# A three-branch encoder layer on eight cores: packed layouts, balanced token blocks, projections run between attention steps

## The chip, the cores and the metric

The kernel runs on the 8 cores of one Trainium2 chip (two dies: cores 0 to 3 and 4 to 7). Each core computes one batch element; nothing is exchanged between cores. The metric is the device time in microseconds of the slowest core. A program on all cores has a second, slower state in some executions, in which the cores of one die (or both) show a lower granted TensorE clock; only fast executions are compared here.

## The reference, cut to what matters

```python
D_MODEL, SEQ, DEC_SEQ, PAST_LEN = 2048, 2048, 64, 1024      # 2048 prompt + 64 sample tokens per core
# input projection columns: fox q,k,v, forget logits, fox gate, conv B, C, h, conv gate, mem q, mem gate
z = jnp.einsum('btd,dn->btn', x, w_in)
# A) forgetting attention, 12 heads x 128
s = jnp.einsum('bqhd,bkhd->bhqk', qi, k) * scale + ci[..., :, None] - cum[:, :, None, :]
s = jnp.where(k_pos[None, :] <= pi[:, None], s, NEG_INF)
o = jnp.einsum('bhqk,bkhd->bqhd', jax.nn.softmax(s, axis=-1), v)
# B) gated causal convolution of width 3, 1536 channels, and its last two inputs as a state output
# C) cross-attention of 4 heads x 256 to 256 memory tokens
# each branch * silu(gate) -> its output matrix; merged by sigmoid gates of x; then W_o and LayerNorm
m = g1 * y_fox + g2 * y_conv + g3 * y_mem
return _layernorm(DN_ALPHA * x + jnp.einsum('btd,de->bte', m, w_o), ln_g, ln_b)
```

The outputs are also the new K, V and log-forget caches and the convolution state (two tokens of 1536 channels, for prompt and sample).

## The kernel before

Heads run one after the other: all projections of a head, then its attention. Each attention tile is a score matmul, on the diagonal a mask matmul, an addition on VectorE, an exponential on ScalarE, a value matmul and a matmul with ones that sums the rows.

```python
TBLK = [(0, 512), (512, 512), (1024, 512), (1536, 512), (2048, 64)]
...
    for h in range(nheads):
        ...  # K, V, Q and gate projections of head h, K transposes
        def issue_S(i):
            ...
            S.add(PE, MM(banks[sb_][0:kn, n0:qn], kl, qT[:, qcol0 + n0:qcol0 + qn], True, not diag),
                  reads=rds + [r_qT[tbidx]], writes=[bankr[sb_]])
            if diag:
                S.add(PE, MM(banks[sb_][0:kn, n0:n0 + kn], identb[0:kn, 0:kn], masknegb[0:kn, 0:kn], False, True),
                      reads=[r_const], writes=[bankr[sb_]])
            ...
        def issue_PV(i):
            ...
            S.add(PE, MM(banks[Ob][:, n0:qn], vv, pt[p][0:kn, n0:qn], first, last),
                  reads=[r_pt[p]] + rds, writes=[bankr[Ob]])
            S.add(PE, MM(banks[Lb][:, n0:qn], onesb[0:kn, :], pt[p][0:kn, n0:qn], first, last),
                  reads=[r_pt[p], r_const], writes=[bankr[Lb]])
```

Second, the end of the convolution stores the state with four transfers whose elements lie 4 bytes at a time in memory; the merge bias is loaded in such a way at the start.

```python
    S.add(SP, DMA(bm[:], I["b_merge"].rearrange("(c p) o -> p (c o)", p=128), allow_slow_non_contiguous=True),
          writes=[r_const], dmasem=dconst)
...
        for j in range(2):
            S.add(SP, DMA(O["cv_p"][j:j + 1, :].rearrange("o (c p) -> p (o c)", p=128), utail[:, j, :],
                          allow_slow_non_contiguous=True), reads=[r_ut], dmasem=d_ut)
            S.add(SP, DMA(O["cv_s"][j:j + 1, :].rearrange("o (c p) -> p (o c)", p=128), ustail[:, j, :],
                          allow_slow_non_contiguous=True), reads=[r_ut], dmasem=d_ut)
```

Each stage allocates its own weight buffers from memory that the stage before releases, and x is loaded with tokens along the partitions and transposed on TensorE.

The softmax here doesn't subtract the row's maximum and nothing guards it: scores larger than these inputs give would overflow.

## Time and profile before

4072.21 us median of three fast runs (4066.46 to 4072.93; a fourth, 4310.36, is slow). The profiled execution had a slow second die, so all is read on core 0 of the undisturbed die, 4045.0 us. The prediction below shows the lines. To them I add an account of core 0: for every matmul, the time from its start to the next start, less columns/2.4 + 2.5 ns (29.4 ns for 64 columns and fewer), the cost that the dense stretches show. What is left over is sorted by its size: a start-to-start of 1.5 to 2.3 times the cost counts as a matmul at half clock, more than that as a wait. The sort goes by size alone and is rough: of the 18.3 us of half clock after, only 7.4 stand where the trace grants half clock (91.5 of the 97.4 before); the rest are short waits.

| core 0, us | before | after |
|---|---|---|
| until the first matmul | 26.0 | 10.5 |
| issue cost of all matmuls | 3390.0 | 3271.7 |
| waits | 511.5 | 61.4 |
| half clock | 97.4 | 18.3 |
| other | 2.4 | 6.3 |
| after the last matmul's start | 17.7 | 17.0 |
| span | 4045.0 | 3385.2 |

### The profile page before, as it was taken

The page shows a single profiled execution, that of the slowest core. Times are in us where ns is not written, and L with a number is a line of the kernel's source. Part 1 is how long each engine was busy: PE and PEld are TensorE (multiplying, and loading weights), DVE is VectorE, ACT ScalarE, POOL GpSimd, SP SyncE. Part 2 cuts the span into 40 slices and gives each one's busy share as a digit, 9 for nine tenths or more (in the row PEclk, how much of TensorE's full clock was granted, in tenths as well). Part 3 has the DMA queues.
Part 4 walks back from the last instruction along what each step waited for, and adds up shares of the span by engine and source line. Part 5 has one row for each costly group of instructions (what it writes and reads, how often), then busy time and mean ns, then how long its engine had stood idle before and what let it go on. Part 6 is the DMA issues. An engine that isn't in the chain of part 4 may idle for free.

```text
span 4605.7 us, 57539 instructions; the slowest of 8 cores (4037.3 to 4605.7 us)
## 1 busy us (share of the span) xinstructions
PE 4112.2 (89%) x20854; PEld 1977.5 (43%) x20854; DVE 840.7 (18%) x1331; ACT 1033.7 (22%) x1840; POOL 786.6 (17%) x675
## 2 busy tenths in 40 slices
PE   4888888888888799999999998599997997999898
PEld 2555545555555344444444443244443443444343
DVE  2222222222221100101111111000000221111254
ACT  2444433444443110111111111011112331111111
POOL 1111111111110000002132131122210111222122
PEclk7999978999997788888888887688877887888787
DMA  8333333333331433632442440955835203665532
GB/s 102 50 53 60 52 43 52 52 52 52 52 52 34 60 63 66 86 43 21 35 37 19 37 33 4 65 106 105 142 86 75 30 8 55 110 121 115 182 132 92
DMA packets 500443, 303.11 MB, mean 66 GB/s; under 512 B 275440, under 2 KB 457456, under 8 KB 494140
## 3 DMA queue, kind: packets, MB, share of 16 engines
q0 software_dynamic: 344080, 134.54, 29.1%
q1 hardware_dynamic: 156088, 164.89, 12.7%
q8 instruction: 174, 2.85, 0.3%
q14 instruction: 101, 0.83, 0.1%
HBM read 345.03 MB, written 88.88 MB: 94 GB/s over the span
## 4 chain that ended last, share of the span: by engine, by line
PE 85%; ACT 5%; DMA 4%; issue 3%; DVE 2%; another core or an unknown queue 1%; DVEq 0%; ACTq 0%; SPq 0%; POOL 0%; POOLq 0%
PE bank L146 84%; ACT rl_92 L163 1%; DMA xb_14_56<-xp 1%; DMA mwb_74_116<-w_in 1%; DMA wm_56_98<-w_merge 0%; PE bank L152 0%; DMA mwb_74_116<-w_mem_kv 0%; DMA wm_107_149<-w_merge 0%; DVE st_41_83 L181 0%; ACT pt_47_89 L163 0%; ACT pt_44_86 L163 0%; ACT pt_45_87 L163 0%; ACT pt_49_91 L163 0%; ACT pt_48_90 L163 0%
## 5 line engine op out<-in xcount | busy, mean ns | idle before, releaser
L146 PE MATMUL bank<-xT_55,cwb_52_94 128*128 128x512 bf16 (+1 forms) x1920 | 418.8, 389 | 3.2 <-ACT scg_114 L163 1.8
L146 PE MATMUL bank<-xT_55,cwb_53_95 128*128 128x512 bf16 (+1 forms) x1920 | 418.8, 389 | 3.2 <-ACT scg_114 L163 2.2
L146 PE MATMUL bank<-wbuf_69,xT_55 128*128 128x256 bf16 (+1 forms) x3264 | 403.5, 290 | 16.1 <-ACT kv_1_34_76 L168 10.7
L146 PE MATMUL bank<-xT_55,wbuf_69 128*128 128x512 bf16 (+1 forms) x1920 | 360.7, 350 | 17.8 <-ACT kT_71 L168 8.5
L146 PEld LDWEIGHTS bank<-wbuf_69,xT_55 128*128 128x128 bf16 (+1 forms) x3264 | 337.3, 104 | 76.5 <-issue 21.6
L146 PE MATMUL bank<-wob_146,mT_159 128*128 128x512 bf16 (+1 forms) x1088 | 287.6, 438 | 21.5 <-DMA mT_159<-m_scrb 21.5
L146 PEld LDWEIGHTS bank<-xT_55,cwb_52_94 128*128 128x128 bf16 x1920 | 180.8, 107 | 240.8 <-issue 240.6
L146 PEld LDWEIGHTS bank<-xT_55,cwb_53_95 128*128 128x128 bf16 x1920 | 180.8, 107 | 240.6 <-issue 240.6
L146 PEld LDWEIGHTS bank<-xT_55,wbuf_69 128*128 128x128 bf16 x1920 | 165.1, 99 | 209.2 <-issue 60.5
L146 PE MATMUL bank<-xT_55,wm_79_121 128*128 128x512 bf16 (+1 forms) x640 | 147.6, 393 | 69.0 <-DMA wm_79_121<-w_merge 69.0
L146 PEld LDWEIGHTS bank<-wob_146,mT_159 128*128 128x128 bf16 (+1 forms) x1088 | 119.5, 110 | 189.1 <-issue 179.2
L146 PE MATMUL bank<-qT_70,kT_71 128*128 128x512 bf16 (+4 forms) x492 | 189.3, 392 | 9.9 <-ACT kcT_81 L168 9.5
L146 PE MATMUL bank<-xT_55,wm_56_98 128*128 128x512 bf16 (+1 forms) x640 | 147.1, 392 | 24.0 <-DMA wm_56_98<-w_merge 24.0
L146 PE MATMUL bank<-xT_55,wm_107_149 128*128 128x512 bf16 (+1 forms) x640 | 147.2, 392 | 23.3 <-DMA wm_107_149<-w_merge 23.3
L163 ACT ACT_TABLE_LOAD x69 | 88.5, 1283 | 328.1 <-PE bank L146 265.1
L173 POOL TENSOR_TENSOR aT_68<-on_93,sg_73 128x512 bf16<-128x512 f32 (+1 forms) x60 | 64.7, 1078 | 553.9 <-DVE on_93 L173 409.8
L146 PE MATMUL bank<-xT_55,mwb_74_116 128*128 128x512 bf16 (+1 forms) x640 | 142.3, 392 | 12.6 <-DMA mwb_74_116<-w_in 10.3
L146 PE MATMUL bank<-xT_55,wm_57_99 128*128 128x512 bf16 (+1 forms) x640 | 145.5, 389 | 0.0
L146 PE MATMUL bank<-xT_55,wm_80_122 128*128 128x512 bf16 (+1 forms) x640 | 145.5, 389 | 0.0
L146 PE MATMUL bank<-xT_55,wm_108_150 128*128 128x512 bf16 (+1 forms) x640 | 145.5, 389 | 0.0
L173 DVE TENSOR_TENSOR up_111<-bank,cg_110 128x512 f32<-128x512 f32 x48 | 33.2, 692 | 611.0 <-PE bank L146 611.0
L146 PE MATMUL bank<-xT_55,mwb_75_117 128*128 128x512 bf16 (+1 forms) x640 | 140.7, 389 | 2.3 <-ACT mqT_137 L168 2.3
(277 smaller groups left out, 4856.6 us busy)
## 6 DMA issues: line engine op xcount, KB each, us to landing
wbuf_69<-w_in POOLq DMA_DIRECT2D x48, 512.0 KB, 12.8
cqb_74<-cum_scr SPq DMA_DIRECT2D x12, 1024.0 KB, 5.6
cwb_52_94<-w_in POOLq DMA_DIRECT2D x24, 512.0 KB, 18.2
cwb_53_95<-w_in POOLq DMA_DIRECT2D x24, 512.0 KB, 17.9
m_scr<-mt_60_102 SPq DMA_DIRECT2D x32, 256.0 KB, 2.1
m_scr<-mt_61_103 SPq DMA_DIRECT2D x32, 256.0 KB, 2.0
pv_85_127<-m_scr SPq DMA_DIRECT2D x32, 256.0 KB, 3.6
pv_86_128<-m_scr SPq DMA_DIRECT2D x32, 256.0 KB, 4.3
```

What stands on the lines that cost most here:

```text
L146: return lambda e: e.matmul(out, lhsT=lhsT, rhs=rhs, start=start, stop=stop)
L163: return lambda e: e.activation(out=out, in_=in_, func=func, **kw)
L173: return lambda e: e.tensor_tensor(out=out, in0=in0, in1=in1, op=op)
```

## The change

The intent: keep TensorE fed all the time. The diff replaces most of the kernel; this is its core, with cuts marked by dots and comments added.

```diff
-TBLK = [(0, 512), (512, 512), (1024, 512), (1536, 512), (2048, 64)]
+TB = [(0, 424), (424, 424), (848, 424), (1272, 420), (1692, 420)]
...
-    ("cv_p", [2, FW]), ("mk_p", [MT, MW]), ("mv_p", [MT, MW]), ("fk_s", [NS, FW]), ("fv_s", [NS, FW]),
-    ("b_merge", [3 * D, 1], F32), ("w_o", [D, D], F32), ("ln_g", [1, D], F32), ("ln_b", [1, D], F32),
+    ("w_mem_out", [16, 128, 8, 128], F32), ("w_merge", [48, 128, 16, 128], F32), ("b_merge", [128, 48], F32),
...
+    def load_next(si):                       # eight weight slots, filled in the order of use
+        key, src, nk = stream[spos[0]]
+        ...
+    for q in range(4):                       # prologue: token block 0 and the first K weights in quarters
+        S.add(POOL, DMA(xT[0][:, 4 * q:4 * q + 4, :], I["xT0"][:, 4 * q:4 * q + 4, :]), writes=[r_xT[0][q]], ...)
+        S.add(POOL, DMA(slots[0][0][:, 4 * q:4 * q + 4, :], stream[0][1][:, 4 * q:4 * q + 4, :]), ...)
...
-            if diag:
-                S.add(PE, MM(banks[sb_][0:kn, n0:n0 + kn], identb[0:kn, 0:kn], masknegb[0:kn, 0:kn], False, True), ...)
+        def fmask():                         # the mask is added to the forget row once, on GpSimd
+                S.add(POOL, TT(m[:, :]..., t[:, :]..., masknegb..., ALU.add), ...)
...
-            S.add(PE, MM(banks[Lb][:, n0:qn], onesb[0:kn, :], pt[p][0:kn, n0:qn], first, last), ...)
+            S.add(DVE, TT(ac[0:kn, n0:n], ac[0:kn, n0:n], p[0:kn, n0:n], ALU.add), reads=[rac, rp], writes=[rac])
+    # at the end of a query block: high and low bf16 parts on GpSimd, two matmuls with ones
+        def f2():
+            bk, rb = PJ.next()
+            E.pe(MM(bk[:, 0:n], onesb[:, :], hi[:, 0:n], True, False), n, [rhi, r_const], [rb])
+            E.pe(MM(bk[:, 0:n], onesb[:, :], lo[:, 0:n], False, True), n, [rlo, r_const], [rb])
...
+    for h in range(H):
+            F.add(*[g_v(h + 1, b) for b in range(5)])     # and K, Q, gate projections of head h + 1
+        for s in ss:
+            step(s)                          # one attention tile of head h
+            F.run(fill * weight(s) / tot)    # then a share of the next head's projections
```

Besides, x and the caches come transposed and the weights packed from the host's preparation, so that TensorE transposes only V; branch results are spilled to memory and read back for the merges; SiLU is built of exponentials beside attention, so that ScalarE's tables stay (70 loads of 1283 ns before).

## The prediction

> **What bounds the kernel now.** I read the core view first. The profiled execution is one in which the second die was slow, so I read everything below on core 0, whose span of 4045.0 us belongs to the timed runs (4066 to 4073 us).
>
> ```profile
> core 0: 4045.0 us, clock 0.950
> core 7: 4605.7 us, clock 0.824
> die 0 (median of its cores): 4049.9 us, clock 0.948
> die 1 (median of its cores): 4564.7 us, clock 0.823
> ```
>
> Next the stage table of core 0: start:end, length, busy time of TensorE, its weight loads, VectorE, ScalarE, GpSimd, then granted clock, DMA share, GB/s. The stages are prologue, attention heads, first merge, convolution (with a gap at its end), second merge, memory keys, memory attention, third merge, output projection.
>
> ```profile
> 0.00:112.67 112.67, 51.96 (x403) 37.84 (x404) 31.76 (x45) 28.04 (x49) 16.91 (x28) 0.72 0.87 105
> 112.67:1466.00 1353.33, 1131.20 (x7437) 683.58 (x7437) 325.54 (x646) 586.54 (x1132) 195.92 (x245) 0.94 0.34 51
> 1943.00:2656.00 713.00, 634.05 (x3555) 297.68 (x3551) 115.83 (x128) 85.86 (x167) 202.02 (x104) 0.95 0.45 34
> 3068.00:3136.00 68.00, 39.44 (x160) 15.88 (x161) 0.00 (x0) 10.90 (x24) 11.56 (x14) 0.75 1.00 143
> 3781.00:4045.00 264.00, 237.35 (x1088) 107.58 (x1088) 141.32 (x204) 41.88 (x35) 76.94 (x17) 0.95 0.50 168
> ...
> 1880.00:2580.00 700.00, 692.59 (x3822) 324.22 (x3821) 112.42 (x128) 94.23 (x179) 189.57 (x100) 1.00 0.36 35
> ```
>
> The reader is to see that TensorE is the bound where work is dense (last line: 692.59 of 700 us at clock 1.00), and that the loss sits elsewhere: in the prologue, in attention, and at stage boundaries. No other engine is near full anywhere. "Busy" overstates TensorE, since each matmul's tail is counted, so I need the true cost of one matmul. The timeline of a dense stretch gives it by start to start:
>
> ```profile
> 1879.70 2.75 PE L146 MATMUL bank<-xT_55,wm_57_99 128*128 128x512 bf16 x12
> 1882.29 2.75 PE L146 MATMUL bank<-aT_68,wo_55_97 128*128 128x512 bf16 x12
> 1884.88 0.63 PE L146 MATMUL bank<-xT_55,wm_57_99 128*128 128x64 bf16 x16
> 1885.35 0.51 PE L146 MATMUL bank<-aT_68,wo_55_97 128*128 128x64 bf16 x12
> ```
>
> (1882.29-1879.70)/12 = 215.8 ns for 512 columns; (1885.35-1884.88)/16 = 29.4 ns for 64. That is 0.4167 ns per column plus about 2.5 ns. Last, who made TensorE wait:
>
> ```profile
> PE bank L146 <- DMA wm_79_121<-w_merge: 74.5, 1, 74.5
> PE bank L146 <- ACT pt_46_88 L163: 29.1, 21, 2.9
> PE bank L152 <- DVE epsb_51 L308: 26.0, 1, 26.0
> PE bank L146 <- DMA mT_159<-m_scrb: 16.5, 1, 16.5
> ```
>
> One 74.5 us wait for merge weights, six pt groups of about 28.7 us each (172 us in all) where the value product waits for the exponential, 26.0 us before the first matmul, 16.5 us before the output projection.
>
> **What the Trainium skill says.** "TensorE: Matmul & The Clock Gate", section "Back-to-back issue gap", gives N/2.4 + 2.5 ns; the 215.8 ns above agrees. Part 1 of the page says that idle time drops the clock to half and that three dense cores of a die bring 13/16: the slow die agrees (0.82), core 0 does not (1.00 for 700 us with all cores busy), so measurement decides: the fast state holds under dense work. "SBUF — State Buffer", section "Who interferes with whom", says that VectorE with two SBUF inputs and a GpSimd operation that reads SBUF exclude each other; the trace agrees with some exclusion: two like GpSimd copies of two elements take 183 and 2104 ns, the long one beside VectorE's convolution sweeps.
>
> ```profile
> L169 POOL COPY ustail_54<-us_112 128x2 f32<-128x2 f32 x12 | 25.2, 2104 | 1.6
> L169 POOL COPY utail_53<-up_111 128x2 f32<-128x2 f32 x12 | 2.2, 183 | 0.0
> ```
>
> "ScalarE: Activation LUTs", section "Table sets", says exp and ln share a set; the trace agrees: Ln and Exp of rl stand back to back in attention with no load of 1283 ns between them. So replacing Silu by Exp/Ln chains beside attention costs no loads.
>
> **The change part by part.** TensorE's work first. One 2112-column pass of a weight block is 4x215.8+29.4 = 892.6 ns before. Balanced blocks (424,424,424,420,420) cost 3x179.2+2x177.5 = 892.6 ns by the same formula: nothing gained in issue, only that 64-column groups no longer outrun their drains (convolution: 58.2 us per channel group against 64x0.8926 = 57.1).
>
> After, at full clock:
> - 112 input blocks and the forget block: 113x16x0.8926 = 1613.8 us.
> - Merge gates: 48x16x0.8926 = 685.5. Branch outputs: (12+12+8)x16x0.8926 = 457.0.
> - Output projection: 1088x0.2158 = 234.8. Memory keys and values: 256 matmuls of 256 columns x0.1092 = 28.0. Memory attention: 4x10x0.8926 = 35.7.
> - Forgetting attention per head: scores 24 full tiles and four diagonals of 512, 384, 256, 128: 24x0.2158+4x0.543 = 7.35; values the same; sample 18x0.0294 = 0.53; row sums now 8x0.2158+2x0.0294 = 1.79; v transposes 17x0.0558 = 0.95. Sum 17.97, times 12 = 215.6.
> - Small transposes 4. Sum 3274 us.
>
> Before: heads cost 25.2 each, because the ones matmul ran per tile (7.35, now moved to VectorE adds), the mask was a matmul (0.9) and the K cache was transposed (0.45); token-major K/V cost 14 us more in all; x was transposed on TensorE (about 25). Sum near 3400. So the removed matmuls are worth some 125 us; the other 645 us of core 0's 4045 are waits and cold clock, and most of the gain has to come from there:
> - Attention: 1353.3 us against 12x83.5 = 1002 us of issue, 351 lost. The new kernel fills these waits with the next head's projections.
> - Prologue: 112.7 us for about 40 of matmuls, 72 lost.
> - The rest, about 220: 74.5 for the merge weights (the new weights buffer is inherited from space still used by the convolution), about 43 in memory keys, 12 to 16 at each merge start, 16.5 before the output, 14 of tail, drains.
>
> **What is left after.** (a) Prologue. A DMA stretch with 1 KB output packets (x loads, 40 to 76 us) moved 156 GB/s at share 0.99, one with 256 B packets (160 to 175 us) 89 GB/s at 0.97. Packed inputs have packets of 3 to 4 KB, so I take 160 GB/s. First x block and K weights, 2.3 MB: 14 us plus about 3 to start. Q, V, f, G, 1.6 MB: to 28 us. The block's five groups at 2.87 us end near 33. Each further x block takes 11 us to arrive against 14.3 (or 11.5) us of matmuls, so from there TensorE is the bound. Lost: 33-14.3 = 19, with cold clock 23. (b) Attention, 75.1 us of TensorE per head. VectorE per head: score adds 27.7 (0.686 per 512, with split diagonals), new accumulations 22.8 (0.69 per 512), silu and normalization 7.9: 58.4, or 78%. ScalarE: exps 23.5, silu chains 9.5, drains 10, row sums 5: 48, or 64%. GpSimd: casts, masks, hi/lo splits, gate products and six DMA issues at 1.15: 32. None binds, but accumulations have two SBUF inputs, and a clash with GpSimd in a third of about 46 such operations at half a microsecond brings VectorE to about 88%. I allow 3.5 us per head: 42. (c) Boundaries: 8 ring slots, each worth 14.3 us of matmuls, loaded in about 4 us; reloads are early. 12 for five boundaries. (d) Tail 9, the start of the last sixty-four rows being split. (e) Slowest core over core 0 and timing overhead: 4072-4045 = 27, I take 25. Sum: 3274+23+42+12+9+25 = 3385 us, a ratio of 0.83.
>
> **The rivals.** First: VectorE becomes the bound in attention. For it: 78% before contention, in-order queue, score ring of two banks. Against: work is issued with 4.6 us of lead before the value product. It would cost 10 us more per head, so 3500. Second: dense work on all cores trips the limiter in every run. For it: the second die's 0.82, its dense stages at 0.81. Against: three timed runs at 4072 with long dense stages. It would make 3274/0.82+110 = 4100, no gain. Third: scratch spills and ring loads make TensorE wait on DMA. Against: shares of 0.3 to 0.7 with small packets. It would make 3450. Fourth: waits vanish wholly, 3320.
>
> **Range and chances.** 80% between 3310 and 3500: the low end is nearly no attention loss, the high end the first rival. Faster by over 2%: 0.95; within 2%: 0.03 (the second rival); slower: 0.02.
>
> **What would show it.** Right: TensorE busy above 95% in all slices after the second; attention near 78 us per head; no single wait over 5 us after the prologue; ScalarE table loads well below 69; x landing before 85 us. Wrong: waits of TensorE on st or the accumulator's VectorE line summing over 100 us; granted clock under 0.95 on both dies; ring weights in the wait list. The weakest step is the 3.5 us per head.

## The result, and the profile after

Correct, 3397.07 us median of 4 runs (3393.39 to 3399.11): 0.834 of the time before, 95% interval 0.833 to 0.836. Ratios are the mean time of one kernel's fast runs over that of the other's of the same rounds, so not quite the ratio of the medians. The prediction was 3385, range 3310 to 3500.

The core view of the changed kernel, for two cores:

```profile
core 0: 3385.2 us, clock 0.997
core 6: 3394.8 us, clock 0.994
```

No die was slow. The page is of core 6; TensorE and its clock in 40 slices (tenths):

```profile
PE   7999999999999999999999999999999999999998
PEclk9999999999999999999999999999999999999999
```

The holes of before are gone: every slice but the first and the last is at 90% or more. The stage table of core 6, in the columns that the prediction explains:

```profile
0.00:26.20 26.20, 4.71 (x13) 1.33 (x13) 2.54 (x4) 0.00 (x0) 18.32 (x38) 1.00 0.92 128
165.00:1018.50 853.50, 831.15 (x4816) 441.00 (x4816) 640.78 (x1202) 532.97 (x998) 311.82 (x426) 1.00 0.38 79
1983.00:3126.00 1143.00, 1143.00 (x6395) 622.73 (x6395) 143.10 (x241) 148.28 (x243) 226.20 (x263) 1.00 0.53 119
3126.00:3150.00 24.00, 18.03 (x74) 7.70 (x73) 2.26 (x4) 1.44 (x3) 5.27 (x6) 0.86 0.83 214
3378.20:3394.80 16.60, 0.00 (x0) 0.00 (x0) 8.04 (x11) 1.11 (x2) 3.31 (x2) 0.64 0.24 72
```

Attention runs at clock 1.00 with VectorE at 640.78/853.5 = 75%; the later convolution, memory and merge stages (third line) have no hole at all. Losses remain at the start, at the change to the output projection (fourth line), and in the tail (fifth). Who made TensorE wait on core 6 (total, times, longest):

```profile
PE bank L148 <- DMA ring_23_65<-w_in: 21.5, 4, 10.8
PE bank L148 <- DMA mT_141_183<-mb_scr: 6.0, 1, 6.0
PE bank L148 <- ACT kv_44_86 L170: 4.5, 6, 0.9
PE bank L148 <- ACT kv_46_88 L170: 4.4, 5, 0.9
PE bank L148 <- ACT qT_77 L170: 3.7, 7, 0.6
```

Against one wait of 74.5 us and six groups of 28 to 29 us before, the longest is the first load. In attention the waits are now on ScalarE's copies of projections (kv, qT), not on VectorE's scores (st), of which the prediction was afraid. Such a wait in TensorE's timeline (start and length in us, xN equal matmuls in a row; in brackets the idle time before and what ended it):

```profile
367.17 0.19 PE L148 MATMUL bank<-hl_84_126,onesb_45 128*128 128x64 bf16 x1
367.20 0.19 PE L148 MATMUL bank<-hl_85_127,onesb_45 128*128 128x64 bf16 x1
...
367.66 0.70 PE L148 MATMUL bank<-xT_18_60,ring_25_67 128*128 128x424 bf16 x3
369.24 1.24 PE L148 MATMUL bank<-xT_19_61,ring_25_67 128*128 128x424 bf16 x6 [0.88 <-ACT kv_44_86 L170]
```

The row sums (hl with ones) use a bank of the same ring of three as the projections (xT with ring). Two short matmuls take up a bank for as long as ScalarE needs to read it, so the next projection group finds its bank not yet copied out.

### The profile page after: what moved, and what is told of

It is laid out like the page before. It is cut to its first block, busy times and chain, and to the rows that moved or that the text cites. A ratio compares the mean times of both kernels' runs of the same rounds, so it can differ in the third digit from the quotient of the medians.

```text
span 3394.8 us, 54855 instructions; the slowest of 8 cores (3381.3 to 3394.8 us)
## 1 busy us (share of the span) xinstructions
PE 3319.9 (98%) x18557; PEld 1775.1 (52%) x18557; DVE 1253.6 (37%) x2239; ACT 1011.5 (30%) x1843; POOL 845.5 (25%) x1035
## 4 chain that ended last, share of the span: by engine, by line
PE 96%; DMA 1%; DVE 1%; ACT 1%; issue 1%; POOL 0%; ACTq 0%; DVEq 0%; SPq 0%; POOLq 0%
PE bank L148 95%; DMA ring_24_66<-w_in 1%; DMA ring_30_72<-w_o 0%; PE bank L154 0%; DVE x_143_185 L183 0%; DVE acc_81_123 L175 0%; ACT qT_77 L170 0%; DMA mb_scr<-gt_116_158 0%; ACT qT_73 L170 0%; DVE acc_80_122 L175 0%; DVE st_71_113 L183 0%; ACT kv_44_86 L170 0%; ACT ge_56_98 L165 0%; ACT kv_46_88 L170 0%; POOL xT_18_60 L157 0%
## 5 line engine op out<-in xcount | busy, mean ns | idle before, releaser
L175 DVE TENSOR_TENSOR mt_118_160<-bank,gt_116_158 128x424 f32<-128x424 f32 (+1 forms) x120 | 71.8, 598 | 526.6 <-PE bank L148 360.4
L175 DVE TENSOR_TENSOR mt_119_161<-bank,gt_117_159 128x424 f32<-128x424 f32 (+1 forms) x120 | 71.8, 598 | 480.4 <-PE bank L148 358.3
L165 ACT ACTIVATE gt_116_158<-bank,bm_50 128x424 f32<-128x424 f32 (+1 forms) x120 | 73.4, 612 | 519.7 <-PE bank L148 370.5
L165 ACT ACTIVATE gt_117_159<-bank,bm_50 128x424 f32<-128x424 f32 (+1 forms) x120 | 73.4, 612 | 481.1 <-PE bank L148 354.7
L148 PE MATMUL bank<-xT_18_60,ring_23_65 128*128 128x424 bf16 x400 | 81.4, 350 | 21.5 <-DMA ring_23_65<-w_in 21.5
L148 PE MATMUL bank<-xT_18_60,ring_24_66 128*128 128x424 bf16 x416 | 85.1, 352 | 1.7 <-DMA ring_24_66<-w_in 1.7
L148 PE MATMUL bank<-xT_19_61,ring_27_69 128*128 128x424 bf16 x432 | 85.9, 345 | 0.0
L148 PE MATMUL bank<-xT_20_62,ring_24_66 128*128 128x424 bf16 x416 | 82.5, 342 | 3.0 <-ACT qT_73 L170 3.0
L148 PE MATMUL bank<-qT_77,kT_78 128*128 128x512 bf16 (+4 forms) x246 | 84.4, 343 | 0.9 <-DVE st_72_114 L183 0.5
L148 PE MATMUL bank<-xT_20_62,ring_29_71 128*128 128x424 bf16 x416 | 82.0, 342 | 3.0 <-ACT qT_77 L170 3.0
L148 PE MATMUL bank<-xT_20_62,ring_27_69 128*128 128x424 bf16 x432 | 84.8, 342 | 0.0
L148 PE MATMUL bank<-qT_73,kT_74 128*128 128x512 bf16 (+4 forms) x246 | 84.5, 343 | 0.3
L148 PE MATMUL bank<-xT_22_64,ring_27_69 128*128 128x420 bf16 x432 | 84.7, 340 | 0.0
L148 PE MATMUL bank<-xT_18_60,ring_27_69 128*128 128x424 bf16 x432 | 84.2, 343 | 0.2 <-ACT kv_44_86 L170 0.2
L148 PE MATMUL bank<-xT_21_63,ring_27_69 128*128 128x420 bf16 x432 | 84.4, 340 | 0.0
L148 PE MATMUL bank<-xT_18_60,ring_29_71 128*128 128x424 bf16 x416 | 83.8, 346 | 0.0
L148 PE MATMUL bank<-xT_19_61,ring_24_66 128*128 128x424 bf16 x416 | 83.1, 342 | 0.0
L148 PE MATMUL bank<-xT_19_61,ring_29_71 128*128 128x424 bf16 x416 | 82.9, 342 | 0.0
L148 PE MATMUL bank<-xT_22_64,ring_29_71 128*128 128x420 bf16 x416 | 81.5, 340 | 1.1 <-ACT qT_77 L170 0.4
L148 PE MATMUL bank<-xT_22_64,ring_24_66 128*128 128x420 bf16 x416 | 81.7, 340 | 0.7
L148 PE MATMUL bank<-xT_21_63,ring_24_66 128*128 128x420 bf16 x416 | 81.8, 340 | 0.0
L148 PE MATMUL bank<-xT_21_63,ring_29_71 128*128 128x420 bf16 x416 | 81.4, 340 | 0.3 <-ACT qT_77 L170 0.3
```

Of the source, the lines that this page charges most:

```text
L148: return lambda e: e.matmul(out, lhsT=lhsT, rhs=rhs, start=start, stop=stop)
L165: return lambda e: e.activation(out=out, in_=in_, func=func, **kw)
L175: return lambda e: e.tensor_tensor(out=out, in0=in0, in1=in1, op=op)
```

## The experiments

Twelve runs, in three calls; in each call all kernels ran on one chip beside runs of the kernel before. The lengths of stages are start-to-start times from the traces: attention from the first value product of head 0 to the last of head 11, output from the last matmul of the merges to the last matmul. Only the first call, with the control, row-sum, mask and doubled-GpSimd runs, held a control; across calls I compare ratios and stage lengths.

**Control.** The changed kernel unaltered.

> The changed kernel once more, unedited, as the control for the three runs beside it. Expected 3397 us within 5 us, a ratio of 0.834 to the kernel before.

Measured: four fast runs, 3389.36, 3389.74, 3393.26 and 3411.66 us (median 3391.5, mean 3396.0), ratio 0.8333 (0.8304 to 0.8361). In the longest, cores 0 and 1 took 272 us for the output, the other complete cores 244 to 250, so this run makes the control's mean some 5 us high. Attention 942.1 us in an issue cost of 899.4.

**Row sums in the score ring.** Is the attention loss the projection ring, or VectorE?

```diff
         def f2():
-            bk, rb = PJ.next()
+            bk, rb = SRING.next()
```

> The two row-sum matmuls of each query block write into the score ring of two banks, not into the projection ring of three. Theory A: the 39.6 us that the attention stretch (165 to 1018 us) takes above its issue time come from short groups (row sums, v transposes) that fall into one projection group, so that the next group needs the bank that ScalarE has only begun to drain. Then about half of it goes: 15 to 25 us less than the control, and the waits of TensorE on the kv and q drains of ScalarE, 15 us together, fall below 6. Theory B (the step of my prediction): VectorE and GpSimd shut each other out and the score adds come late. Then nothing changes, within 4 us of the control.

Measured: 3372.5 us, ratio 0.8275 (0.8256 to 0.8295); 19 us less than the control by the medians (3391.5), 23 by the means (3396.0). Attention falls by 18.9, from 942.1 to 923.2 us, and the waits on kv are gone. What remains on core 6, after the loads:

```profile
PE bank L148 <- DVE st L183: 3.6, 10, 1.1
...
PE bank L148 <- ACT qT L170: 1.1, 6, 0.4
```

So nearly half of attention's loss (18.9 of 42.7 us) was the shared ring, with VectorE's load unchanged. The theory of the ring holds; the 23.8 us that remain are many small waits (the largest group, on st, some 5 us), which no run takes apart.

**The mask back on TensorE.**

```diff
-        E.pe(MM(sb[0:kn, n0:n], kl, qT[i][:, t0 + n0:t0 + n], True, True), nn, rks + rq, [rs])
+        E.pe(MM(sb[0:kn, n0:n], kl, qT[i][:, t0 + n0:t0 + n], True, not diag), nn, rks + rq, [rs])
 ...
         if diag:
-            n1 = n0 + kn
-            S.add(DVE, STT(x[0:kn, n0:n1], sb[0:kn, n0:n1], SCALE, cm[0:kn, n0:n1], ALU.mult, ALU.add), ...)
+            E.pe(MM(sb[0:kn, n0:n0 + kn], identb[0:kn, 0:kn], masknegb[0:kn, 0:kn], False, True), kn, [r_const], [rs])
```

> The causal mask goes back to TensorE as a matmul of the mask by the identity into the score bank, as in the kernel before; GpSimd loses its mask adds (about 6 us per head) and VectorE one small add per diagonal tile. Theory A (TensorE issue is the bound): 16x55.8 ns and one of 29.4 more per head, 0.92 us, times 12 = 11 us more than the control. Theory B (VectorE with GpSimd holds attention up): both get lighter by several us per head, and the time falls by 10 to 40 us.

Measured: 3411.7 us, ratio 0.8377 (0.8356 to 0.8398). Attention's issue cost grows by 10.8 us (899.4 to 910.2), its length by 14 (942.1 to 956.5), though GpSimd and VectorE have less to do. TensorE's own work sets the pace; taking this work off the others earned nothing.

**GpSimd's row-sum and gate work twice, then the gate product alone twice.**

```diff
+            S.add(POOL, TT(lo[:, 0:n], ac[:, 0:n], hi[:, 0:n], ALU.subtract), reads=[rac, rhi], writes=[rlo])   # first run only
...
-                S.add(POOL, TT(a[...], o[...], sg[b][...], ALU.mult), reads=[r, r_sg[b]], writes=[ra])
+                for _ in range(2):
+                    S.add(POOL, TT(a[...], o[...], sg[b][...], ALU.mult), reads=[r, r_sg[b]], writes=[ra])      # both runs
```

> GpSimd does the gate product and the low-part subtraction of each query block twice, same result: about 11 us more of SBUF-reading GpSimd work per head on 29. Theory A: GpSimd has room, VectorE's adds stretch a little, the time rises by less than 8 us over the control. Theory B: the 3.5 us per head grow with GpSimd's busy time, by at least 15 us in all, more likely 20 to 60.

Measured: 3452.5 us, ratio 0.8477 (0.8455 to 0.8499); attention 1003.7 us, 62 more. By size this looks like contention, but the list of TensorE's waits on core 6 names something else:

```profile
PE bank L148 <- POOL hl L175: 46.6, 47, 2.5
```

The doubled low part (hl) sits in front of the row-sum matmul, which is queued a fixed 2.8 us of work later, and TensorE stood still for it in 47 places. The experiment mixed two costs, so I repeated it without that part.

> The changed kernel with only the gate product on GpSimd done twice (about 118 us more GpSimd work over the whole attention stretch on one core by the run with both doubled, 5.4 of it per doubled head's worth of single products, that is some 55 to 60 us in all), and not the low part of the row sums, which TensorE waits for. Theory A (attention is bound by TensorE and by the projection ring; GpSimd's load costs nothing unless it is in a chain that TensorE waits for; the 61 us that the run with both doubled lost came from the doubled low part in front of the row-sum matmul): attention stays within 942 to 950 us, waits of GpSimd's low part stay near zero, time 0 to 8 us more. Theory B (shared access of VectorE and GpSimd to memory stretches VectorE, which stalls the scores): attention grows by 20 to 35 us, with VectorE's waits on scores' banks grown in proportion.

Measured: fast runs of 3406.68 and 3408.76 us (two more were slow, so there is no interval); attention 959.3, 17 more than the control. Both expectations miss: the one said 0 to 8, the other 20 to 35. VectorE's waits in attention show why, first in the control (core 6), then here (core 1):

```profile
DVE on L175 <- POOL ao L175: 5.2, 10, 0.5
```

```profile
DVE on L175 <- POOL ao L175: 31.4, 15, 2.3
```

The normalized block (on) has one buffer. VectorE may not write the next one before GpSimd's gate product (ao) has read it, and while VectorE waits there, the scores behind it in its queue wait too: TensorE's waits on st rise from 2.8 to 14.8 us. VectorE's accumulations themselves stretch from 731 to 757 ns only. So the trace points to a buffer that came free late, with contention between the two engines small; a run with a second buffer, which would prove it, was not made. (Another 11.9 us of VectorE's waits before this block are put down to ScalarE's gate exponentials, ge.)

**The interleaving undone.** The few groups that a head's attention still needs, then its attention alone, then all other projections of the next head.

```diff
+        for _ in range(2 if h == 0 else 4 if h + 1 < H else 3):
+            runall(F.q.popleft())
 ...
             step(s)
-            F.run(fill * weight(s) / tot)
+            E.tick(fill * weight(s) / tot)
+        F.finish()
```

The expectation puts all projections ahead of the attention; they stand between two attentions either way. The work is the same, 3271.7 us of issue.

> The changed kernel with one part of the change undone: the projections of the next head are all run before the attention of a head, not between its steps. Theory A (the main gain of the change is that VectorE's and ScalarE's attention work, 58.7 and 49.6 us of a head's 78.1 us, lies beside projection matmuls): a head then takes its projections' issue (about 57 us) and, after that, an attention that VectorE bounds at about 45 us, some 102 us instead of 78.8, so over the heads 240 to 300 us more, 3640 to 3720 us in all: about the 331 us that the attention stretch gained over before. Theory B (the gain of attention came from the packed layouts and balanced blocks rather than from the order): less than 100 us more.

Measured: two fast runs, 3854.58 and 3869.08 us (three were slow); ratio 0.9468 (0.9425 to 0.9510). That is some 460 us more, above both expectations. On core 1 a head takes 117.4 us on average (score matmuls begin at 233.6, 350.1, 468.5, ...), of which its attention alone takes 55.5 where the expectation had 45. TensorE's waits and two stretches of 10 us, one among projections and one in attention:

```profile
PE bank L148 <- DVE st L183: 130.4, 153, 1.6
PE bank L148 <- ACT pt L165: 62.7, 187, 1.3
```

```profile
430.00:440.00 10.00, 10.00 (x63) 5.66 (x62) 0.00 (x0) 3.06 (x6) 1.58 (x3) 1.00 0.46 95
...
490.00:500.00 10.00, 7.41 (x17) 1.61 (x15) 9.74 (x16) 6.19 (x11) 4.74 (x7) 0.50 0.06 15
```

Alone, attention is VectorE's: 9.74 of 10 us busy here, 88 to 91% over three whole attentions (50.87 of 55.6 us in the first), while TensorE waits in pieces of at most 1.6 us. That went with a granted clock of 0.50; the 7.41 us of TensorE are 17 matmuls at that clock. Whole-kernel account of core 1: waits 421 us (61 in the changed kernel), half clock 119 (18). Note also that 117.4 us is more than the 113.0 us per head of the kernel before (core 0, worked out in the same way): without projections in between, the new head is slower than the old one, though TensorE has less to issue in it (75.1 against 83.4 us). The row sums that moved to VectorE are the likeliest reason, but the heads also differ in mask, SiLU and layouts, and no run puts the row sums back: that these two parts of the change earn only together is argued, not shown.

**Start of the kernel: holding back later loads, and no quarters.**

```diff
     load_next(3)
+    S.add(POOL, COPY(gate0[0:1, 0:2], xT[0][0:1, 8, 0:2]), reads=[r_xT[0][2]], writes=[r_gate0])
     for b in range(1, 5):
         load_x(b)
```

> The changed kernel with one thing added: GpSimd copies two numbers out of the third quarter of token block 0 before it issues the loads of blocks 1 to 4, so that these 2 MB each do not start while block 0 and the first K weights are still landing. Theory A (later transfers share the transfer engines with earlier ones, so the first quarters land late because 3.3 MB move in 26 us where 2.3 MB are needed): the quarters' first matmuls come earlier than 10.8, 16.3, 20.3 and 26.2 us, the last by 4 to 8 us, block 1 still arrives before TensorE has used up block 0, and the kernel is 4 to 8 us shorter than the control. Theory B (the engines serve transfers in the order of their issue, as the prediction had it): the quarters' times do not change, and the time is the same or a little longer because blocks 1 to 4 start later.

Measured: 3390.0 us, ratio 0.8322 (0.8291 to 0.8353), the control's 0.8333 within the interval. The loads of blocks 1 to 4, issued from 8 us on in the changed kernel, are issued from 20.7 us on. On core 6 the quarters' matmuls start at 10.76, 17.12, 20.91 and 28.14 us, not earlier than in the changed kernel. So blocks 1 to 4 do not delay the first loads; my theory falls, and the prediction's order of service is not contradicted. The Q, V and gate weights, issued just behind block 0, and the small constants on SyncE's queue were not held back.

```diff
-    runall(proj(("K", 0), 0, g_k(0, 0, True), rq=r_k0))
+    for k in range(16):
+        E.pe(MM(bk0_[...], w0_[:, k, :], xT[0][:, k, 0:TB[0][1]], k == 0, k == 15), TB[0][1], [rw0_] + r_xT[0] + r_k0, [rb0_])
```

> The changed kernel with the first K group waiting for all four quarters of token block 0 and of its weights, as if they were one transfer. Theory A (the transfers bound the start, and the quarters let TensorE do three of four quarters of this group's 2.8 us in waits): the end of the first K group moves from about 28 us to about 29 to 30 us, time 1 to 3 us more, which the interval does not resolve. Theory B (quarters matter more, since the clock stays up or the later groups start earlier): over 6 us.

Measured: 3395.3 us, ratio 0.8332 (0.8310 to 0.8355), no difference. TensorE's timeline of core 0, in the changed kernel and here:

```profile
10.49 1.57 PE L148 MATMUL bank<-xT_18_60,ring_23_65 128*128 128x424 bf16 x4 [10.49 <-DMA ring_23_65<-w_in]
...
25.56 1.57 PE L148 MATMUL bank<-xT_18_60,ring_23_65 128*128 128x424 bf16 x4 [3.82 <-DMA ring_23_65<-w_in]
28.84 2.63 PE L148 MATMUL bank<-xT_18_60,ring_24_66 128*128 128x424 bf16 x7 [1.71 <-DMA ring_24_66<-w_in]
```

```profile
25.83 10.42 PE L148 MATMUL bank<-xT,ring 128*128 128x424 bf16 x46 [25.83 <-DMA ring<-w_in]
```

With quarters, three quarters of the first group are done early, but the next group then waits for its own weights until 28.84. Without them the first group runs from 25.83 for 2.87 us, to about 28.7, and the next follows without a wait. The quartering is hidden by the load behind it.

**Weights in their natural layout** (pieces of 512 bytes in memory instead of 4 to 8 KB; x packed as before).

```diff
-    def win(key, ch):
-        put(key, I["w_in"][ch], 16)
+    def nat(w, o):
+        return w[:, o:o + 128].rearrange("(c p) n -> p c n", p=128)
+    def win(key, ch):
+        put(key, nat(I["w_in"], SECO[ch]), 16)
```

> The changed kernel with the weights left in their natural order (pieces of 512 bytes instead of 3 to 8 KB), x packed as before. Theory A (after the prologue every weight is loaded 8 slots ahead, so that the packing of weights earns only in the prologue): the prologue, up to the first value product, is 3 to 20 us longer, the attention stretch and the merges within 5 us, no wait of TensorE for ring weights after the prologue beyond 2 us. Theory B (packing pays throughout, the transfer engines being shared with spills): ring waits appear in the merge stage, and the time grows by over 40 us.

Measured: 3419.1 us, ratio 0.8393 (0.8369 to 0.8416), some 24 us more than the run without quarters beside it. Up to the first value product the cores take 108 to 130 us from their first matmul, where the control takes 101 to 103: 6 to 28 us more, the upper end beyond my 20 (and the first matmul itself is some 2 us later). Attention (942.3 to 943.3 us) and the merges are as before. On core 0 the loss is mostly one wait for weights (core 5 has nine such waits, 56.0 us with those that the changed kernel has too):

```profile
52.53 4.83 PE L148 MATMUL bank<-xT,ring 128*128 128x424 bf16 x16 [13.10 <-DMA ring<-w_in]
```

Here packing the weights pays only where loads are on the path, in the prologue.

**The last two output weights earlier.**

```diff
-                if tb == 4:
-                    Wfree(("WM", u, j), 0.3 if last and j == 15 else 2.5)
-                    Wfree(("WO", u, j), 0.3 if last and j == 15 else 2.5)
+                if tb == 4 and last and j == 15:
+                    load_next(where.pop(("WM", u, j)))
+                    load_next(where.pop(("WO", u, j)))
```

> The changed kernel with the last two output weights' loads emitted before the last add of the merge stage instead of 0.3 us of work after it. In the changed kernel TensorE waits 3.7 us for the one of them at the start of the output projection and 6.0 us for the last block of the merged activations. Theory A (the weight's wait is a late issue): the 3.7 us wait goes, the output stage's loss over issue falls from 9 to 15 us by 2 to 4 us, time 2 to 5 us less than the control. Theory B (the wait is only hidden behind the one for the merged activations and the cold clock after it, or the transfer is slow there): the time is within 1.5 us of the control.

Measured: 3385.6 us, ratio 0.8300 (0.8278 to 0.8323). The run beside it on the same chip whose edit did nothing, the held-back loads, has a fast median of 3390 us, so about 4 us less, as theory A had it; all four fast runs (to 3386.92) lie under all five of its neighbour (from 3387.90). The output stage takes 240.6 us (mean of the six cores with complete records), in the run beside it 244.1, in the changed kernel's profile 247.8. The last two have the same output stage and differ as much, so the length alone proves nothing; but the waits for output weights (ring from w_o) fall from 2.7 to 6.0 us on the eight cores of the neighbour to 0 to 2.1. The intervals of the ratios overlap.

**The kernel before with two scattered transfers packed.** Where did the 74.5 us at the end of its convolution come from?

```diff
-            S.add(SP, DMA(O["cv_p"][j:j + 1, :].rearrange("o (c p) -> p (o c)", p=128), utail[:, j, :], ...
-            S.add(SP, DMA(O["cv_s"][j:j + 1, :].rearrange("o (c p) -> p (o c)", p=128), ustail[:, j, :], ...
+        S.add(SP, DMA(O["cv_p"], utail[:].rearrange("p a b -> p (a b)")), reads=[r_ut], dmasem=d_ut)
+        S.add(SP, DMA(O["cv_s"], ustail[:].rearrange("p a b -> p (a b)")), reads=[r_ut], dmasem=d_ut)
 ...
-    S.add(SP, DMA(bm[:], I["b_merge"].rearrange("(c p) o -> p (c o)", p=128), allow_slow_non_contiguous=True),
+    S.add(SP, DMA(bm[:], I["b_merge"]),
```

> The kernel before with two things of the change alone: the convolution's four last-token stores are laid out per partition (96-byte pieces instead of 4-byte ones), and the merge bias is loaded in such a layout as well. Theory A (the 74.5 us wait for merge weights at the end of the convolution is mostly the four stores of 4-byte packets, 6144 of them, that hold the transfer engines at 1 to 20 GB/s from 2590 to 2630 us, and only 16 us of it are the buffer that comes free late, the weights being issued at 2600.65): the wait falls to 28 to 40 us, and with a few us to some 15 us at the start of the kernel the whole is 40 to 60 us shorter. Theory B (the prediction's: the new weights buffer is inherited from space that the convolution uses): the wait stays at 70 to 75 us, and the whole gains only what the start gains, under 20 us.

Measured: two fast runs, 4024.04 and 4025.69 us (two slow); the six fast runs of the kernel before have a mean of 4076.7, so 52 us less. The stretch on core 0 in the kernel before, then with the packed stores (last columns: clock, DMA share, GB/s; a share over 1 counts packets that overlap in time):

```profile
2600.00:2610.00 10.00, 0.00 (x0) 0.00 (x0) 0.00 (x0) 0.00 (x0) 5.02 (x5) 0.50 2.25 5
2610.00:2620.00 10.00, 0.00 (x0) 0.00 (x0) 0.00 (x0) 0.00 (x0) 0.00 (x0) 0.50 1.81 13
```

```profile
2600.00:2610.00 10.00, 0.00 (x0) 0.00 (x0) 0.00 (x0) 0.00 (x0) 3.61 (x4) 0.50 1.25 196
2610.00:2620.00 10.00, 5.57 (x15) 2.00 (x16) 0.00 (x0) 0.00 (x0) 0.00 (x0) 0.52 1.45 195
```

In both, GpSimd issues the weight loads at about 2600 us. Before, all transfers together move 5 and 13 GB/s beside 24 KB of stores in 4-byte pieces; packed, 196 GB/s. The longest wait falls from 74.5 to 31.4 us, and the wait before the first matmul from 26.0 to 19.4:

```profile
PE bank L146 <- DMA wm<-w_merge: 63.8, 3, 31.4
PE bank L152 <- DVE epsb L308: 19.4, 1, 19.4
```

Theory A holds. Of the 31.4 us that remain, some 16 pass before the loads are issued (behind GpSimd's last two products of the convolution, 4.63 us each); the rest is the transfer.

**A better version: the row sums in the score ring and the earlier weights together.**

> The changed kernel with the row sums in the score ring and the last two output weights' loads emitted earlier. If the gains of the two add (attention 942 to 923 us, output stage's loss 3 to 10 us less): 3360 to 3368 us, a ratio to before of 0.824 to 0.826. If the earlier weights only uncover the wait for the last merged block: 3370, as with the row sums alone.

Measured: three fast runs of 3369.82 to 3371.13 us (three were slow), ratio 0.8267 (0.8246 to 0.8288). Attention takes 923.2 us, so the first gain is there whole. Beside the run with the row sums alone (fast mean 3372.7, output 245.0 us) the earlier weights add only about 2 us (3370.3, output 243.3), so the second expectation is the nearer one. On different chips 2 us are not resolved. It is the fastest kernel, 21 us ahead of the changed kernel by the fast medians (3370.1 against 3391.5 of the control), 26 by the means.

## Why the prediction was right

Its sum, term by term, against the profiled run of the changed kernel (core 0; 3396.3 us):

| term | predicted | measured |
|---|---|---|
| TensorE's issue cost | 3274 | 3271.7 |
| (a) prologue | 23 | 34 (10.5 to the first matmul, 23.2 after) |
| (b) attention | 42 | 43.4 |
| (c) boundaries | 12 | 19.5 (5.5 in all stages between, 14.0 at the output) |
| (d) tail | 9 | 17.0 |
| (e) slowest core and overhead | 25 | 11.1 (3396.3 - 3385.2) |

- **TensorE's issue and the bound.** Right to 2 us. The view that carried it was start-to-start times in a dense stretch, not "busy".
- **(b) Size right, cause wrong.** 78.6 us per head were predicted; the changed kernel has 78.1 to 78.8. VectorE's 58.4 per head was right as well (58.70 in one head). But the 3.5 us per head were allowed for VectorE's contention with GpSimd. The row-sum run shows nearly half of the loss (18.9 of 42.7 us) to be the three-bank ring that row sums share with projections. In the control TensorE's waits on st, where late score adds would show, come to 2.8 us, and with the gate product doubled VectorE's accumulations lengthen by 26 ns of 731. What the other 23.8 us are is open. That predicted and measured loss agree is luck.
- **(a) Too small by 11.** I put block 0 and the K weights, 2.3 MB, at 17 us; their last quarter was used at 25.6 on core 0. I took 160 GB/s from 3 us on; up to 26.2 us core 6 moved 128 GB/s on average. Holding blocks 1 to 4 back changed nothing, so most of the error is the rate at which these 2.3 MB arrive. At that mean rate 2.3 MB would take 18 us; why they are complete only then, and how much of it the Q and V weights behind them take, is open. The quartering, in which the reader may see the remedy, is hidden.
- **(c) and (d)** were too small: the merged activations and output weights come late at the last boundary, and the tail, nearly twice the 9 us, hardly shrank (17.7 before, 17.0 after). **(e)** was too large and cancels half of the other errors; that is luck too.
- **Where the gain came from.** The prediction said that the 74.5 us stood for a weights buffer inherited from the convolution's space. That step is wrong for 43 us of it, which were stores in 4-byte pieces on the transfer engines; a late issue, which an inherited buffer would explain, accounts for some 16 at most. "The new kernel fills these waits" was right and, by the run without interleaving, worth some 460 us in the changed kernel, well above my estimate of 240 to 300: I had VectorE bound attention alone at 45 us where it took 55.5, and left out that TensorE's clock would drop.
- **The rivals.** VectorE as the bound: refuted as built, but that is what comes without the interleaving. The limiter in every run: refuted, clock 0.994 to 0.997 in the profiled run, though core 6 shows three stretches of 15.1 us at 0.81 (from 1777.8, 1847.1 and 1914.9 us). Waits on transfers: only in the prologue and at the output.
- **The tests named there.** Attention near 78 us per head, table loads 5, x in time: met. "TensorE above 95% in all slices after the second" was missed in the slice of the last boundary (78.93 of 84.9 us, 93%) and in the tail's, the last; "no single wait over 5 us after the prologue" there too (6.0 us). One sign of being wrong came in small: ring weights in the wait list after the prologue, 3.7 us at the output.

## What to carry to other kernels

Fill the waits of a bound-by-several-engines stage with independent matmuls before trimming the stage: here that was worth more than all else, and moving work to VectorE probably pays only together with it (argued, not shown). Look whether short matmul groups share a bank ring with long ones: here separating them earned 19 us. Look for small scattered transfers wherever a wait on a large load is unexplained, and ask of every early load whether the next one hides it.

## What the Trainium skill lacked or had wrong

- "TensorE: Matmul & The Clock Gate", Part 1: it has the whole die at 13/16 of the clock once three of its cores run dense matmuls. All eight cores had a mean of 0.994 to 0.998 over 3.39 ms in the four fast runs that gave the result (TensorE 98% busy on core 6, with three stretches of 15.1 us at 0.81). Slow executions agree better with the page: one die at 0.811 to 0.813 in the slowest of the runs with plain weights.
- The same part ties the half clock to an idle window of about 3.4 us, and mentions further on that frequent micro-idles make the clock swing, without saying how long they are. Without interleaving, waits of at most 1.6 us, spread over attention, went with a granted clock of 0.50.
- The same page, section "Back-to-back issue gap": about 131 ns per matmul of 512 columns in a sustained stream. The streams here take 215.8 ns, the formula that the page calls isolated (its Part 1 measures 215.7 back to back itself).
- "DMA: Bandwidth & Descriptors", section "Specifications": pieces under 512 bytes miss line rate. It says that an engine takes turns between its queues packet by packet, but has no figure for what small pieces cost a transfer on another queue: beside four stores of 6 KB in 4-byte pieces, 3.5 MB of weights on another queue and all else moved at 5 and 13 GB/s, which cost TensorE 43 us.
